# A hybrid decoder layer on one core: the first output projection moves behind the paired products, and eight more gates are computed in pairs

## The chip, the cores and the metric

The kernel runs on one core of a Trainium2 chip. The metric is the device time of one execution in microseconds, the median of three runs. The engines are called by the profile's names: PE is TensorE (matmuls; PEld its weight loads), DVE is VectorE, ACT is ScalarE, POOL is GpSimd and SP is SyncE, which here only issues DMAs. POOL issues DMAs too.

## The reference

One inference step of one layer, for a prompt of 512 tokens and 8 single sample tokens, 520 columns in all, at a model width of 2048:

```
sh1, sc1, g1, sh2, sc2, g2 = ada_mod(c, w_ada, b_ada)        # silu(c) @ w_ada + b_ada, split in six
h = modulate(rmsnorm(x, norm1_w), sh1, sc1)
mq, mk, mv, mo, mi, mf, fq, fk, fv, ff, ga, gb = split(h @ w_in + b_in)
y_m = mlstm_output(mlstm(mq, mk, mv, mi, mf), mo, m_hnorm_w)  # 4 heads, width 1024
y_f = forgetting_attention(rmsnorm(fq), rmsnorm(fk), fv, ff)  # 8 heads, width 1024, with a paged cache
merged = sigmoid(ga) * (y_m @ w_proj_a) + sigmoid(gb) * (y_f @ w_proj_b)
x = x + g1 * (merged @ w_out)
h2 = modulate(rmsnorm(x, norm2_w), sh2, sc2)
x = x + g2 * conv_ffn(h2)
```

All of it is in 32-bit floats. `ga` and `gb` are the two gates, 2048 rows each, that is 16 blocks of 128 rows each. y_m @ w_proj_a is the first projection.

## The kernel before, in words

**Layout.** Activations lie with features on the 128 partitions and the 520 columns in the free dimension. A product keeps 32-bit accuracy by splitting both operands into a rounded high part and the rest (`wh`, `wl` of a weight; `hh`, `hl` or the two halves of one tile of an activation), and by three matmuls: high by high, high by low, low by high.

**Two ways to multiply.** `dense` (line 197) computes one block of 128 output rows: for each 128 of the input features it issues 3 x 2 matmuls of 260 columns, 96 for an input width of 2048 and 48 for 1024. Each 1024 columns of weights are loaded by SP into a `raw` tile (seven buffers), cast by ACT into `wh`, and subtracted by DVE into `wl` (three buffers each). `Pair` (line 246) computes two blocks of 128 rows over 2048 features at once, as a 2 by 2 by 2 block product by Winograd's scheme: 7 products of 24 matmuls, 168 in all, where two dense blocks take 192. For that DVE adds weight tiles (four sums a pair) and splits seven weight forms, and the activations are needed in seven forms, `hX[1]` to `hX[7]`. The order of a pair's products is 1, 5, 6, 3, 7, 2, 4.

**What sets the order.** `run_pairs` (line 326) writes the order of the pairs out by hand, with a table of late steps at numbered products. In the dense stretches a list `bg` holds small steps; `dense` runs one of them after each 128 input features (`step`), and one entry of a list `pending` at some of its weight splits (`due`). Elsewhere a scheduler places the instructions of each engine, in an order that is then fixed: each engine, and the DMA queue of SP and of POOL, runs its list in order and waits where an operand or a buffer isn't ready.

**The stages around the change**, with the names that the change touches:

1. The start: the condition's products `ada` (a third of `w_ada` at once), the norm, and a first part `pre` of the projections.
2. The first mixer (mLSTM): 14 dense blocks over `h`, with the four heads' steps as `bg`. The last head's steps `m_tokens` and `m_out` (line 1178) run on into two blocks of the first gate (`w_gate`, line 1222), which only finish them. `m_out` leaves y_m as 16 resident tiles `ya`. From here `pending` holds the products of `w_ada` for SC2, two input blocks at a time.
3. The first projection, `pa`: 16 dense blocks over `ya` (line 1484). Two of them are multiplied by their gates by DVE; 14 are copied by ACT to tiles `pao` and stored by POOL to DRAM (`dmg`). After every second block `h_sums` (line 1242) builds the pairs' forms of one feature block: DVE adds high and low parts of `h` to `hu`, forms four sums, and splits them with ACT into `hf` tiles. Forms 5 and 6 stay; 7 and 4 go to DRAM (`dxf`) and are loaded again by POOL (line 1515, 16 DMAs) when the tiles of `ya` are free.
4. The pairs: 21 units, being 8 of queries and keys, 4 of values and 9 of gates: gate blocks 2 to 15 of `ga` and four of `gb`. A gate pair of `ga` loads the stored `pa` blocks (SP) and DVE multiplies them by the gates. SP loads and PE multiplies one block of `w_ada` for SH2 in each of 16 units (`late_load`, `late_product`).
5. The second mixer (forgetting attention): 12 dense blocks of `gb` (line 1762) as cover, 192 steps, under eight heads of attention and the sample tokens' cache: POOL gathers rows of keys `kp` and values `vp`, DVE multiplies and reduces `kp` to scores `sc`, and the attention's own chain runs over PE (`fS`, `fPT`, `fy`), DVE (`fs`, `sm`) and ACT. The gates' blocks leave through ACT (bias, `sgm`) and a store by POOL (`dsg`).
6. The second projection, `pb`: 16 dense blocks over `yf` (line 1939). The gates come back from `dsg`, 12 of them get their sigmoid here, and the sum with `dmg` becomes `merged`.
7. w_out in pairs, and the feed-forward, in pairs too.

## Time and profile before

| what | value |
|---|---|
| median of 3 runs | 2859.26 us (2858.5 to 2859.64) |
| the profiled execution, its own time | 2862.7 us |
| its span | 2861.0 us |
| PE busy in the span | 2825.4 us, 99% |
| DVE busy | 2154.0 us, 75% |
| ACT busy | 1360.5 us, 48% |
| POOL busy | 413.3 us, 14% |
| mean granted clock of PE | 0.997 |
| moved by DMA | 531.44 MB, mean 186 GB/s |

A row of the windows view gives a stretch of the span, and for each engine the busy time in it with the number of instructions that start there; then the granted clock as a share of full speed, the busy share of the DMA engines, and GB/s. A row of the timeline has a start, a duration, engine, line, operation, output and inputs, and in brackets the idle time before it and what ended that. A row of a tile's view has minimum, median and maximum duration in ns. Matmuls overlap, so a matmul's duration is longer than the step from one to the next.

### The profile page before, as it was taken

What the parts mean: (1) busy time and instruction counts of PE and PEld (TensorE: products, weight loads), DVE (VectorE), ACT (ScalarE), POOL (GpSimd) and SP (SyncE); (2) the same over time, 40 slices, a digit from 0 to 9 for tenths busy, and PEclk for the clock granted to TensorE, in tenths of its full rate; (3) what the DMA queues carried; (4) which work ended last, traced back from release to release, by engine and by line L of the source; (5) the groups of instructions that cost most, each with busy time, mean ns of one, the idle gap of its engine ahead of it and who ended that gap; (6) DMA issues with size and microseconds to landing.
All of it is one profiled execution on the core that took longest, in us unless ns stands there. A gap on an engine that the chain in (4) does not pass through costs nothing.

```text
span 2861.0 us, 57607 instructions
## 1 busy us (share of the span) xinstructions
PE 2825.4 (99%) x23318; PEld 2711.8 (95%) x23318; DVE 2154.0 (75%) x3318; ACT 1360.5 (48%) x2131; POOL 413.3 (14%) x687
## 2 busy tenths in 40 slices
PE   8999999999999999999999999999999999999999
PEld 6888998999999989799999999999999999999999
DVE  5986764676777759468888887878787888788787
ACT  4335543455455544444555444444444445544543
POOL 0001110211100145402111010101010101100100
PEclk9999999999999999999999999999999999999999
DMA  9946657945555578576772344444343346745753
GB/s 339 308 143 201 232 178 261 302 166 188 195 182 175 182 246 270 183 235 208 216 249 93 127 143 129 156 130 159 129 146 117 127 141 188 208 155 169 189 160 104
DMA packets 226755, 531.44 MB, mean 186 GB/s; under 512 B 30304, under 2 KB 83024, under 8 KB 226488
## 3 DMA queue, kind: packets, MB, share of 16 engines
q1 hardware_dynamic: 187296, 426.89, 46.2%
q0 software_dynamic: 38752, 100.64, 11.5%
q8 instruction: 183, 3.00, 0.4%
q14 instruction: 84, 0.69, 0.1%
q10 hardware_dynamic: 440, 0.23, 0.0%
HBM read 451.28 MB, written 72.92 MB: 183 GB/s over the span
## 4 chain that ended last, share of the span: by engine, by line
PE 85%; DVE 5%; issue 5%; DMA 2%; ACT 2%; POOL 1%; SPq 0%; POOLq 0%; DVEq 0%; ACTq 0%
PE x L60 33%; PE y L60 17%; PE z L60 8%; PE gate L213 4%; PE pre L60 3%; PE fo L60 3%; PE pa L213 3%; PE mo L213 2%; PE adp L60 2%; PE mv L213 2%; PE adp L409 1%; DVE wl L60 1%; PE mq L213 1%; PE mk L213 1%; ACT wh L60 1%
## 5 line engine op out<-in xcount | busy, mean ns | idle before, releaser
L60 DVE TENSOR_TENSOR wl<-raw,wh 128x1024 fp32r<-128x1024 f32 (+1 forms) x666 | 802.1, 1205 | 353.3 <-ACT wh L60 348.6
L60 ACT CAST wh<-raw 128x1024 fp32r<-128x1024 f32 (+1 forms) x666 | 689.5, 1036 | 754.7 <-DVE raw L60 386.3
L60 PE MATMUL x<-bf,wh 128*128 128x260 f32 x2624 | 475.2, 282 | 2.1 <-DVE tg L60 2.1
L60 DVE TENSOR_TENSOR raw<-raw,raw 128x1024 f32<-128x1024 f32 x339 | 413.7, 1220 | 5.8
L60 PEld LDWEIGHTS x<-bf,wh 128*128 128x128 f32 x2624 | 403.3, 188 | 2.2 <-ACT wh L60 2.2
L60 PE MATMUL x<-bf,wl 128*128 128x260 f32 x1312 | 370.0, 282 | 0.0
L60 PEld LDWEIGHTS x<-bf,wl 128*128 128x128 f32 x1312 | 246.8, 188 | 0.0
L60 PE MATMUL y<-bf,wh 128*128 128x260 f32 x1312 | 238.2, 282 | 0.0
L60 PEld LDWEIGHTS y<-bf,wh 128*128 128x128 f32 x1312 | 201.6, 188 | 0.0
L168 DVE TENSOR_TENSOR wl<-raw,wh 128x1024 fp32r<-128x1024 f32 x92 | 113.1, 1229 | 107.8 <-ACT wh L167 105.0
L60 PE MATMUL x<-ff,wh 128*128 128x260 f32 x1024 | 186.1, 283 | 0.0
L60 PE MATMUL x<-hf,wh 128*128 128x260 f32 x1008 | 185.4, 284 | 0.0
L60 PE MATMUL y<-bf,wl 128*128 128x260 f32 x656 | 184.7, 282 | 0.0
L167 ACT CAST wh<-raw 128x1024 fp32r<-128x1024 f32 x92 | 96.4, 1048 | 162.0 <-DMA raw<-in_w_in 43.4
L60 PEld LDWEIGHTS x<-hf,wh 128*128 128x128 f32 x1008 | 155.0, 188 | 13.4 <-issue 7.5
L60 PEld LDWEIGHTS x<-ff,wh 128*128 128x128 f32 x1024 | 157.6, 188 | 0.0
L60 PE MATMUL x<-ff,wl 128*128 128x260 f32 x512 | 144.6, 282 | 0.0
L60 PE MATMUL x<-hf,wl 128*128 128x260 f32 x504 | 142.2, 282 | 0.0
L60 PE MATMUL fo<-fe,wh 128*128 128x260 f32 x768 | 125.6, 284 | 1.1 <-DVE fo L60 0.9
L60 PEld LDWEIGHTS y<-bf,wl 128*128 128x128 f32 x656 | 123.5, 188 | 0.0
L60 PE MATMUL z<-bf,wh 128*128 128x260 f32 x656 | 120.9, 284 | 0.0
L60 PEld LDWEIGHTS fo<-fe,wh 128*128 128x128 f32 x768 | 105.6, 188 | 2.5 <-DVE fo L60 2.1
(642 smaller groups left out, 7076.9 us busy)
## 6 DMA issues: line engine op xcount, KB each, us to landing
raw<-in_w_fi SPq DMA_DIRECT2D x176, 512.0 KB
raw<-in_w_in SPq DMA_DIRECT2D x155, 512.0 KB
ar<-in_w_ada SPq DMA_DIRECT2D x192, 256.0 KB
raw<-in_w_ada SPq DMA_DIRECT2D x96, 512.0 KB
raw<-in_w_fo SPq DMA_DIRECT2D x64, 512.0 KB
raw<-in_w_out SPq DMA_DIRECT2D x32, 512.0 KB
raw<-in_w_fo SPq DMA_DIRECT2D x32, 384.0 KB
dff<-cc POOLq DMA_DIRECT2D x44, 260.0 KB
```

Of the source, the lines that this page charges most:

```text
L60: return lambda *a, **k: self.tc.keep_in_program_order(getattr(self.eng, op)(*a, **k))
L167: S.copy(wh[:, :n], raw[:, :n])
L168: V.tensor_tensor(wl[:, :n], raw[:, :n], wh[:, :n].bitcast(F32), op=ALU.subtract)
L213: T.matmul(acc[:, z, :HN], a[:, o], b[:, z * HN:(z + 1) * HN], start=(k == 0 and i == 0), stop=(k == K - 1 and i == 2))
L409: ins = T.matmul(ps[32 * g:32 * g + 32, :], cs[:, k, :], w, start=first, stop=last, tile_position=(0, 32 * g))
```

## The change

- **The first projection** leaves its place ahead of the pairs. `m_out` now stores y_m to DRAM (`dya`, 16 DMAs of POOL), and the 16 `pa` blocks run in the second mixer as cover, behind four dense blocks of `gb`. Their operand comes back in 16 loads by POOL into the buffers of `h`, which is used last by the fourth of those blocks. The gates of `ga` go to DRAM as sigmoids (`dsa`), SP fetches them two blocks ahead (`fetch_a`), DVE multiplies them by the block, and POOL stores the product (`dmg`).
- **Eight more gates in pairs:** all of `gb` but four blocks (12 instead of 4), so 13 gate pairs and 25 units. The gate pairs neither load nor multiply `pa` any more. The dense blocks in the second mixer's cover are now 4 of `gb` (64 steps) and 16 of `pa` (128 steps), 192 steps as before.
- **The forms of the pairs** are built in the first mixer: `h_whole`, `h_sums` and `h_parts` for each of eight feature blocks, one call at every eighth step. The low parts are subtracted by POOL, no longer by DVE, and all four forms go to DRAM. Forms 5 and 6 are loaded during the last head's steps, 7 and 4 at the pairs' start.
- **SC2's products** leave the two gate blocks and the first projection and join SH2's in the pairs: 32 in place of 16, some from tiles `ar` of another pool with four DMAs each.

The matmuls of 128x260 fall from 21350 to 21254; no other count of PE changes.

```diff
     def step():
         f = bg.pop(0) if bg else None
         if f:
             f()
+        n_step[0] += 1
+        if side and n_step[0] % 8 == 0:
+            side.pop(0)()
...
-            ya.append(split(sp, "s", t, "ya"))
+            for g, p in enumerate(split(sp, "s", t, "ya")):
+                G.dma_start(dya[4 * H.i + 2 * e + g][:, :N], p[:, :N])
...
+    def h_whole(i):
+        hu[i] = [pt("hu") for _ in range(2)]
+        for t, c in zip(hu[i], (i, 8 + i)):
+            V.tensor_tensor(t[:, :N], h[c][0][:, :N].bitcast(F32), h[c][1][:, :N].bitcast(F32), op=ALU.add)
...
+    def h_parts(i):
+        b11, b12, b21, b22 = (t[:, o:o + HN] for t in hu.pop(i) for o in (0, HN))
+        for q, f in enumerate((b11, b22, b12, b21)):
+            t = pt("hf", F32R)
+            hi, lo = parts_of(t)
+            S.copy(hi, f)
+            G.tensor_tensor(lo, f, hi.bitcast(F32), op=ALU.subtract)
+            G.dma_start(dxf[8 * q + i][:, :N], t[:, :N])
+    def load_form(n):
+        for i in range(8):
+            t = st("hf", F32R)
+            G.dma_start(t[:, :N], dxf[8 * FORMS.index(n) + i][:, :N])
+            hX[n][i] = parts_of(t)
+    side += [on(f, i) for i in range(8) for f in (h_whole, h_sums, h_parts)]
...
-    pending += ada_steps(SC2)
-    calls[:] = 0, 1, 2
-    NB2 = 4
+    NG = 2
+    NB2 = 12
...
-                if g < KC:
-                    V.tensor_tensor(t, t, self.pa[e][:, o], op=ALU.mult)
-                G.dma_start((dmg[g] if g < KC else dsg[g - KC])[:, o], t)
+                G.dma_start((dsa[g] if g < KC else dsg[g - KC])[:, o], t)
...
+    slots = []
+    for u in range(1, len(units) - 3):
+        slots.append((7 * u + 3, 7 * u + 6, False))
+        if u > 2 and not isinstance(units[u], QueryPair):
+            slots.append((7 * u + 6, 7 * u + 10, True))
+    for q, (ta, tb, by_pt) in enumerate(slots[:2 * KC]):
+        late(ta, late_load, q, by_pt)
+        late(tb, late_product, q)
...
+    h = None
+    ya = [[hp.tile([P, 528], F32R, tag="hl", name=nm("ya")) for _ in range(2)] for _ in range(8)]
+    for i, ts in enumerate(ya):
+        for g, t in enumerate(ts):
+            G.dma_start(t[:, :N], dya[2 * i + g][:, :N])
...
+    for j in range(KC):
+        acc = dense(I["w_pa"][j], ya, "pa")
+        t = ga.pop(j)
+        V.tensor_tensor(z2(t), acc, z2(t), op=ALU.mult)
+        G.dma_start(dmg[j], t[:, :N])
+        fetch_a(j + 2)
```

Three places of the order follow. First, POOL at the start of the pairs, before: `dxf` and `hf` are the forms, `dmg` from `pao` the stores of the first projection.

```order
L1502 DMA dmg_5242<-pao_6630 128x520
L1258 DMA dxf<-hf_6647 128x520
L1258 DMA dxf<-hf_6651 128x520
L1515 DMA hf_6786<-dxf 128x520
L1502 DMA dmg_5242<-pao_6712 128x520
L1515 DMA hf_6788<-dxf 128x520
```

The same place after: `dya` are the last head's stores of y_m, `dsa` the store of the second gate block.

```order
L1528 DMA dsa_2514<-sgm_5627 128x520
L872 DMA lfg<-in_cache_logf,idx_l 128x8
L1191 DMA dya<-yah_5664 128x520
L1191 DMA dya<-yal_5665 128x520
L1191 DMA dya<-yah_5672 128x520
L1191 DMA dya<-yal_5673 128x520
L1528 DMA dsa_2514<-sgm_5784 128x520
L1235 DMA hf_5787<-dxf 128x520
```

The first reload of form 7 stood behind stores of forms and projections; it now stands behind the four stores of the last head's output and behind the store of the last gate block.

Second, POOL in the second mixer around the third and fourth gate block, before: `kp` are the gathers of keys, `fql` and `fkl` low parts of the attention's queries and keys.

```order
L868 DMA kp_12878<-in_cache_k,idx_2452 128x512
L225 TENSOR_TENSOR fql_12744<-fi_12479,fqh_12743 128x512
L225 TENSOR_TENSOR fkl_12748<-fi_12480,fkh_12747 128x512
L1767 DMA dsg_5547<-sgm_12751 128x520
L868 DMA kp_12959<-in_cache_k,idx_2456 128x512
```

The same place after: `ya` are the loads of the projection's operand. Ten more of them, alike, are left out between the last `ya` shown and the gather.

```order
L872 DMA kp_12924<-in_cache_k,idx_2452 128x512
L1787 DMA ya_13018<-dya 128x520
L1787 DMA ya_13019<-dya 128x520
L1787 DMA ya_13020<-dya 128x520
L229 TENSOR_TENSOR fql_12790<-fi_12525,fqh_12789 128x512
L1787 DMA ya_13021<-dya 128x520
L229 TENSOR_TENSOR fkl_12794<-fi_12526,fkh_12793 128x512
L1787 DMA ya_13022<-dya 128x520
L1782 DMA dsg_5450<-sgm_12797 128x520
L1787 DMA ya_13023<-dya 128x520
...
L872 DMA kp_13005<-in_cache_k,idx_2456 128x512
```

All 16 loads stand between two gathers of keys, and the gathers that follow wait behind them.

Third, DVE in the second mixer where the fifth cover block begins, before: `wl` is a weight's low part, `fvl` and `fpl` low parts of values and probabilities.

```order
L60 TENSOR_REDUCE sc<-kp_12781 128x4
L225 TENSOR_TENSOR fpl_13012<-fPT_13006,fph_13011 128x384
L225 TENSOR_TENSOR fpl_13026<-fPT_13022,fph_13025 128x256
L60 TENSOR_TENSOR kp_12878<-kp_12878,qb_12875 128x512
L60 TENSOR_TENSOR kp_12959<-kp_12959,qb_12957 128x512
L168 TENSOR_TENSOR wl_13302<-raw_13299,wh_13301 128x1024
L60 TENSOR_REDUCE sc<-kp_12878 128x4
L225 TENSOR_TENSOR fvl_13078<-vtp_13072,fvh_13077 128x384
```

And after: `ga` is a gate, multiplied by the block `pa`.

```order
L229 TENSOR_TENSOR fpl_13108<-fPT_13104,fph_13107 128x256
L60 TENSOR_REDUCE sc<-kp_12923 128x4
L60 TENSOR_TENSOR kp_12924<-kp_12924,qb_12921 128x512
L168 TENSOR_TENSOR wl_13395<-raw_13392,wh_13394 128x1024
L60 TENSOR_REDUCE sc<-kp_12924 128x4
L1800 TENSOR_TENSOR ga_13050<-pa_13054,ga_13050 128x520
L229 TENSOR_TENSOR fvl_13160<-vtp_13154,fvh_13159 128x384
L60 TENSOR_TENSOR kp_13005<-kp_13005,qb_13003 128x512
```

One multiplication of 520 columns per `pa` block stands on DVE between the attention's steps, and the first gather that was queued behind the loads is the second operand after it.

More of the change, by code (lines that the diff above doesn't have):

```diff
@@ new lines, in tile_hybrid_step, with run @@
+    assert len(slots) >= 2 * KC
+    for q, (ta, tb, by_pt) in enumerate(slots[:2 * KC]):
+        late(ta, late_load, q, by_pt)
+        late(tb, late_product, q)
+        if q % KC == KC - 1:
+            late(tb + 2, late_turn, (SC2, SH2)[q // KC])
+    t0 = 7 * (len(units) - 2)
+    late(t0 + 1, root_load)
+    late(t0 + 3, root_make)
+    late(t0 + 6, rows_load)
+    late(t0 + 8, rows_make)
+    late(t0 + 9, lambda: (hX.pop(5), f_load(heads[0])))
+    late(t0 + 13, f_norm, heads[0])
+    def run(fs):
+        for f in fs:
+            f()
@@ L1747, in tile_hybrid_step @@
         put(183 if hh < FH - 1 else 188, y_sample, hh)
-    def run(fs):
-        for f in fs:
-            f()
     assert not bg
```

149 lines of the change are left out of this document (65 added, 84 removed).

## The prediction

> **What bounds the kernel now.** The page comes first: it says which engine fills the span.
>
> ```profile
> span 2861.0 us, 57607 instructions
> PE 2825.4 (99%) x23318; PEld 2711.8 (95%) x23318; DVE 2154.0 (75%) x3318; ACT 1360.5 (48%) x2131; POOL 413.3 (14%) x687
> ```
>
> PE is busy for all but 35.6 us. A share over the whole span says nothing of single stages, so the windows view is cut at the stages' borders: the first mixer, the two gate blocks, the first projection, the pairs, the second mixer (from 22 us after its start) and the second projection.
>
> ```profile
> 193.60:422.50 228.90, 228.43 (x1770) 207.27 (x1770) 159.56 (x337) 123.43 (x227) 33.68 (x52) 1.00 0.61 198
> 422.50:450.00 27.50, 27.50 (x230) 24.35 (x229) 12.32 (x20) 10.67 (x13) 0.00 (x0) 1.00 0.61 204
> 450.00:555.30 105.30, 105.30 (x874) 95.86 (x873) 56.03 (x101) 38.29 (x64) 20.06 (x37) 1.00 0.83 275
> 555.30:1004.10 448.80, 448.80 (x3724) 433.20 (x3723) 321.56 (x351) 236.17 (x361) 58.82 (x110) 1.00 0.57 188
> 1026.00:1219.60 193.60, 187.47 (x1414) 168.67 (x1415) 128.86 (x315) 87.26 (x188) 92.20 (x90) 0.98 0.69 229
> 1219.60:1311.00 91.40, 91.40 (x769) 91.40 (x768) 69.64 (x113) 42.39 (x66) 11.25 (x22) 1.00 0.63 200
> ```
>
> In the stages that the change takes apart PE has no idle time at full clock; only the second mixer shows some, 6.1 us. So a matmul less is time less, unless a new wait takes it back. The chain of waits gives the pace inside stages, start and duration of merged pieces.
>
> ```profile
> 458.01 11.72 PE pa L213 x96
> 471.59 11.72 PE pa L213 x96
> 659.38 5.95 PE x L60 x48
> 680.66 5.95 PE x L60 x48
> 961.32 5.75 PE x L60 x48
> 981.42 5.75 PE x L60 x48
> ```
>
> Each piece marks the same point of a period. Two `pa` blocks with one step of SC2's products (two input blocks) take 13.58 us; a pair with one SH2 product takes 21.28; a late pair without one takes 20.10.
>
> **The change, term by term.** First PE's work.
>
> 1. The first projection's stage goes: -105.3 us. Its 768 matmuls reappear in the second mixer, where they replace the 768 of eight gate blocks one for one: 0.
> 2. The gate blocks lose two SC2 steps. The second projection has 16 blocks in 91.4 us, 11.43 for two, so a step costs 13.58 - 11.43 = 2.15 us: -4.3.
> 3. Four more pairs, 4 x 20.1 = +80.4.
> 4. SC2's 16 products in the pairs at 21.28 - 20.10 = 1.18 each: +18.9.
>
> The sum is -10.3 us. Against it stand waits that can be new, at four places.
>
> **The first mixer.** The forms' building moves here. The prices are in the tile views (min, median, max in ns), in the groups of POOL, in the timeline where DVE and POOL run side by side, and in the ten-us windows, of which the first and the last of eight crowded ones stand here.
>
> ```profile
> L1246 DVE TENSOR_TENSOR hu<-hh,hl x16: 690/693/695, 442.7 to 545.8; 128x520 f32<-128x520 f32 x16
> L1248 DVE TENSOR_TENSOR hu<-hu x8: 420/422/423, 445.1 to 546.4; 128x260 f32<-128x260 f32 x8
> L225 POOL TENSOR_TENSOR fkl<-fi,fkh 128x512 fp32r<-128x512 f32 x8 | 10.3, 1287 | 0.0
> 1083.65 0.68 DVE L60 TENSOR_TENSOR kp<-kp,qb 128x512 f32<-128x512 f32 x1
> 1087.10 2.00 DVE L60 TENSOR_TENSOR kp<-kp,qb 128x512 f32<-128x512 f32 x2
> 1086.66 1.29 POOL L225 TENSOR_TENSOR fkl<-fi,fkh 128x512 fp32r<-128x512 f32 x1
> 210.00:220.00 10.00, 10.00 (x84) 8.27 (x84) 8.60 (x24) 2.94 (x4) 1.32 (x2) 1.00 0.73 263
> 400.00:410.00 10.00, 10.00 (x78) 9.75 (x77) 8.79 (x19) 6.21 (x17) 1.11 (x2) 1.00 0.53 170
> ```
>
> DVE gets eight blocks of 2 x 0.693 + 4 x 0.422, 24.6 us, over 192 steps. With 159.6 of 228.9 us busy it goes to 184, 80%. ACT gets 32 casts and has 105 us free. POOL gets 32 subtractions; scaled from 512 to 260 columns one is an estimated 0.65 us, 21 us in all, with 64 DMA issues that wait only for data. Two multiplications on DVE that POOL's subtraction overlapped took 2.00 us, not 2 x 0.68, so up to half of POOL's time can fall on DVE: 10 us, at the outside all 21, and then DVE is at 205 of 229, 90%. The cover is the three buffers of split weights, each some 6 us of PE. In eight of the ten-us windows DVE is busy for 8.5 us or more, between 8.53 and 9.79; adding 1.25 and 1.07 us to each overfills them by 10 us in sum. So the cost lies between 0 and 10 us. I take 0.5, near the low end, since PE waits nowhere in this stage now. Below 0 it can't go: there is no idle time to win.
>
> The Trainium skill ("SBUF — State Buffer", section "Who interferes with whom") says that a DVE instruction with two inputs in SBUF is shut out by a GpSimd instruction that reads SBUF, for the whole of it. The stretched pair above agrees. By that rule taken strictly the cost would be the outer end just named, and moving the subtractions to POOL would win DVE little; it is the first rival below.
>
> **The start of the pairs.** Form 7 is needed at the fifth product, 4 x 2.87 (20.10 / 7) = 11.5 us in, form 4 at the seventh, 17.2 us in, one tile each 0.36 us. The rows are POOL's first and last reload, the same stretch in the DMA view, DVE's `m_out`, and a reload of this sort before the next set of pairs.
>
> ```profile
> 550.55 0.55 POOL L1515 DMA_DIRECT2D hf<-dxf  x1
> 562.66 0.54 POOL L1515 DMA_DIRECT2D hf<-dxf  x1 [0.60 <-DMA hf<-dxf]
> DMA packets 3185, 7.00 MB, mean 333 GB/s; under 512 B 365, under 2 KB 365, under 8 KB 3182
> 438.62 0.76 DVE L363 SCALAR_TENSOR_TENSOR rv<-ms,rd 128x260 f32<-128x260 f32 x2
> 449.28 0.69 DVE L225 TENSOR_TENSOR yal<-hm,yah 128x520 fp32r<-128x520 f32 x1
> 1310.93 10.09 DMA mf<-dxf
> ```
>
> The reloads (16 x 266 KB, 4.26 MB) began 4.75 us ahead of the pairs at 555.3; in 550 to 571 the DMAs moved 7.0 MB at 333 GB/s. Now they stand on POOL behind the stores of `m_out`'s output and of the last gate. `m_out` ran from 438.6 to 450.0, 11.4 us; the second gate block takes 11.4 us without SC2's step, so it ends about at the pairs' start, four issues of 0.55 and the gate's activation come next, and the reloads begin some 3 us in, 8 us later than now. At 277 GB/s (4.26 MB in the 15.4 us that the saturated stretch took) the last tile lands near 3 + 2 + 15.4 = 20.4 us, against a need at 17.2 + 7 x 0.36 = 19.7. Cost 0 to 8 us (all of the shift); I take 1. The same sort of reload before the output pairs took 10.1 us from issue to landing and held PE up for about 1 us. Behind the reloads on POOL stand the first query pair's stores, whose data come later still.
>
> **The pairs themselves.** DVE is at 72% and loses 28 multiplications; SP loses 14 loads of `pa` and gains SC2's weights, 16.8 MB over more than 400 us, some 40 GB/s on 188. Loads into `ar` tiles wait for stores of the unit before, and weight loads stand behind them on SP, but those are wanted two or more products later. Cost 0, bounded by one product, 2.87 us.
>
> **The second mixer.** Its rows: POOL around the third and fourth gate block (the `dsg` stores follow their ends), the MB that SP's queue moves in 1004.1 to 1219.6, the price of a multiplication by a block, DVE's load after that, and a spell of idle time.
>
> ```profile
> 1059.74 0.95 POOL L868 DMA_INDIRECT kp<-in_cache_k,idx  x1 [0.30 <-issue]
> 1064.14 0.59 POOL L1767 DMA_DIRECT2D dsg<-sgm  x1
> 1074.84 0.99 POOL L868 DMA_INDIRECT kp<-in_cache_k,idx  x1 [10.12 <-DVE fs L1579]
> 1077.70 0.57 POOL L1767 DMA_DIRECT2D dsg<-sgm  x1
> q1 hardware_dynamic: 11485, 27.60, 40.1%
> L1971 DVE TENSOR_TENSOR sgm<-pb,sgm x16: 690/693/700, 1225.6 to 1311.5; 128x520 f32<-128x520 f32 x16
> 1070.00:1140.00 70.00, 69.61 (x554) 66.96 (x553) 64.33 (x148) 34.19 (x75) 37.35 (x36) 1.00 0.80 265
> 1004.00:1010.00 6.00, 6.00 (x48) 5.66 (x47) 2.26 (x5) 5.21 (x9) 2.82 (x6) 1.00 0.74 241
> 1022.00:1028.00 6.00, 4.03 (x29) 3.31 (x28) 6.00 (x22) 3.33 (x8) 2.04 (x3) 1.00 1.02 391
> 1028.00:1034.00 6.00, 3.15 (x15) 3.15 (x16) 4.04 (x9) 1.88 (x4) 3.53 (x4) 0.65 0.90 280
> 1034.00:1040.00 6.00, 6.00 (x39) 5.84 (x39) 2.68 (x4) 3.66 (x8) 1.94 (x2) 0.78 0.56 185
> ```
>
> The loads of `ya` wait for PE's last reading of `h`, by the fourth gate block, from about 1062 to 1077. POOL reaches them after the gather at 1059.7 and then has nothing to do until 1074.8, so they fit where they are. Their 4.26 MB share the DMAs with 265 GB/s; at 333 in all, and 128 (27.60 MB in 215.5 us) for SP's queue, while POOL's own gathers wait behind, they take about 21 us from 1064, so the last is there near 1085. PE wants it seven eighths into the first `pa` block, some 7 us after 1077: a wait of about 1 us. The gathers behind them land later by up to that stretch, and DVE waits for those in its order.
>
> DVE also multiplies 16 blocks, 16 x 0.693 = 11.1 us. Eight fall into 1070 to 1140, where it is busy for 64.3 of 70 us: 64.3 + 8 x 0.69 = 69.9. That is full. What a late DVE costs stands in the windows from 1022 to 1040: 4.8 us idle, and the granted clock falls to 0.65 and 0.78 after it, so 83 matmuls start where 144 would at the pace of 1004 to 1010; at 0.125 us that is 7.6 us. I take 2.5 us for this stage, between -6.1 (all its present idle time, but DVE's and SP's rows at its start are unchanged) and 15.
>
> All terms: -10.3 + 0.5 + 1 + 0 + 2.5 = -6.3. The profiled execution took 2862.7 us, 3.4 above the median of the runs; its 2856.4 corresponds to 2853.0 on the median. 5.7 us, 0.2%, is about what a measurement of this kernel can tell from no change.
>
> **The rivals.**
>
> - *The first mixer becomes DVE's* (chance 0.07). For it: eight crowded windows and the stretched multiplications; against: no wait of PE there today and 20% of slack on DVE even with the forms. Price 10 in place of 0.5: 2853.0 + 9.5 = 2862.5.
> - *DVE overfills in the second mixer* (0.14). For it: 69.9 of 70 us; against: weights are split two and three blocks ahead. One more spell like the one at 1025 replaces the 2.5: 2853.0 + 7.6 - 2.5 = 2858.1; two of them make 2865.7.
> - *The forms come late* (0.07): 8 in place of 1, 2860.0. For it, the shift by 8 us against a slack of a few; against, the first tile is wanted only 11.5 us in.
> - *The projection's operand comes late, and the kernel is slower* (0.10). If POOL hangs in the key gathers in front (they wait for buffers that DVE frees, as in the 10.12 us at 1074.8) and reaches the `ya` loads only when the fourth gate block ends, PE waits for 21 of stream less the 7 that the first block needs anyway, 14 us, and 3 for the clock: 17 in place of 2.5, 2867.5. It decides when POOL is some 9 us late: 9 and 3 for the clock are the 6.3 and 5.7 us that lie between my sum and slower.
> - *The fewer matmuls save nothing*: excluded by the windows, since PE never waited in the pairs.
>
> **How the numbers follow.** My own case has 0.62 and a range of 2847 to 2855.5: the net of -10.3 with stalls of 2 to 6.5, or less if the mixer's own idle time shrinks. Of that 0.54 lies under 2853.5, faster, and 0.08 within 0.2%. The first three rivals, 0.28, end within 0.2%; the fourth, 0.10, slower. So 0.54, 0.36, 0.10. The range runs from 2846 to 2864, over my case and the first three rivals; left out are the late operand and the tails.
>
> **What would show it.** Right: no stage between 450 and the pairs; pairs 25 units long with PE busy throughout, near 548 us (448.8 + 80.4 + 18.9); the two gate blocks in about 23; 0 to 2 us of waits of PE for `hf` and `ya` each. Wrong: POOL's first reload of form 7 over 5 us after the pairs' start; the first `ya` load after the fourth gate block's middle; a dip of the granted clock in the second mixer beyond the one at its start; DVE above 90% in the first mixer with PE waiting for `wl`. If PE's time falls by other than 10 us, terms 1 to 4 are wrong; if it falls and the span doesn't, a wait is.

## The result, and the profile after

The changed kernel is slower: 2897.33 us as the median of four runs (2896.16 to 2903.63) against 2859.11 us, a ratio of 1.0138 with a 95% interval of 1.0121 to 1.0156. Run again later beside other kernels it gave 1.0124 (1.0107 to 1.0141). The forecast was 2853.0, faster; 2864 was the top of its range. The trace below is of the execution of 2903.63 us, the longest of the four; where a second number is given, it is from the trace of the later repeat (2895.93 us).

First the page of the changed kernel, the lines that answer to those of before.

```profile
span 2901.6 us, 57751 instructions
PE 2841.4 (98%) x23222; PEld 2717.9 (94%) x23222; DVE 2194.6 (76%) x3312; ACT 1363.6 (47%) x2141; POOL 480.7 (17%) x793
```

PE is busy for longer than before, 2841.4 us, with fewer matmuls. So part of what was lost is matmuls that ran slowly, and PE's idle time grew as well, from 35.6 to 60.2 us. The windows at the same stages say where: the first mixer, the two gate blocks, the pairs, the second mixer from 21 us after its start, and the second projection.

```profile
193.60:444.20 250.60, 239.39 (x1807) 216.62 (x1806) 195.37 (x388) 134.85 (x260) 83.54 (x127) 0.98 0.70 227
444.20:467.50 23.30, 23.30 (x196) 23.30 (x195) 10.29 (x13) 9.47 (x11) 5.73 (x10) 1.00 0.63 201
467.50:1024.00 556.50, 553.32 (x4536) 520.79 (x4536) 374.78 (x388) 278.70 (x422) 72.35 (x136) 0.99 0.60 197
1045.00:1257.00 212.00, 197.22 (x1414) 172.93 (x1414) 137.00 (x330) 83.02 (x181) 104.66 (x114) 0.95 0.78 260
1257.00:1348.90 91.90, 91.90 (x771) 91.90 (x770) 70.58 (x114) 37.24 (x57) 11.71 (x22) 1.00 0.62 202
```

The first mixer is 21.7 us longer than before (5 of these are the start's: the mixer's first matmul, of `mo`, comes at 198.7 us, before at 193.7), the gate blocks 4.2 shorter, the first projection's 105.3 are gone, the pairs are 107.7 longer (99.3 were forecast), the second mixer from the end of the pairs to the second projection takes 233 in place of 215.5, 17.5 longer. Three stages lost what the matmuls gained.

In the first mixer PE now waits, in few and long pieces. These are its waits between 193.6 and 444.2 (waiting line, what for, us in total, times, longest).

```profile
PE ms L390 <- DVE hi L381: 4.5, 1, 4.5
PE ms L390 <- ACT hf L1228: 2.3, 1, 2.3
PE ktp L1151 <- DVE dl L1039: 1.9, 1, 1.9
```

They are the mixer's own chains: `ms` sums the squares in `m_out`, `ktp` turns the keys. What may stand in front of them is one queue further back, in SP's waits and in DVE's for the state (`c`, loaded by SP at line 1108, after; line 1105 before). SP's waits in the first mixer after:

```profile
SPq L1108 <- POOL hf L1229: 6.2, 1, 6.2
SPq L1108 <- DMA dxf<-hf: 4.6, 2, 3.0
SPq L1102 <- DMA dxf<-hf: 3.0, 2, 2.7
```

DVE's wait for that load, first after, then before:

```profile
DVE tmp L1111 <- DMA c<-in_state_C: 20.9, 8, 5.1
```

```profile
DVE tmp L1108 <- DMA c<-in_state_C: 8.1, 9, 1.6
```

The forms' tiles `hu` and `hf` come from the same nine buffers as the mixer's state, so SP can't load the state until a form has been stored, and DVE stands in its order until the state is there. These rows don't show how much of this reaches PE; the experiments below ask that.

A wait can cost more than its length. The windows around the one at 329 us show it; the last three columns are granted clock, DMA share and GB/s.

```profile
328.00:332.00 4.00, 1.46 (x11) 1.07 (x9) 3.15 (x12) 3.12 (x7) 1.18 (x2) 1.00 0.35 126
332.00:336.00 4.00, 3.97 (x19) 3.88 (x20) 3.96 (x6) 3.11 (x5) 3.98 (x5) 0.57 0.32 62
336.00:340.00 4.00, 4.00 (x34) 3.72 (x32) 3.67 (x5) 3.99 (x9) 3.31 (x4) 1.00 0.90 266
```

2.5 us of idle time, then four microseconds in which PE is busy but starts 19 matmuls in place of 34.

In the second mixer PE's waits are these:

```profile
PE sO L1701 <- DMA vp<-in_cache_v,idx: 6.9, 6, 5.3
PE fPT L1609 <- DVE fs L1598: 5.0, 2, 3.6
PE pa L217 <- DMA ya<-dya: 2.7, 5, 0.9
```

The second row was there before (5.2). The first is new at this size (0.4 before): the sample tokens' attention (`sO`) waits for gathered values. In POOL's timeline just ahead of that wait, the eight gathers in a row cut to their first and last:

```profile
1181.84 0.59 POOL L1801 DMA_DIRECT2D dmg<-ga  x1 [2.61 <-DVE ga L1800]
1182.55 1.28 POOL L229 TENSOR_TENSOR fql<-fi,fqh 128x512 fp32r<-128x512 f32 x1
1183.79 1.27 POOL L229 TENSOR_TENSOR fkl<-fi,fkh 128x512 fp32r<-128x512 f32 x1
1185.22 1.00 POOL L872 DMA_INDIRECT vp<-in_cache_v,idx  x1 [0.16 <-issue]
...
1194.59 0.97 POOL L872 DMA_INDIRECT vp<-in_cache_v,idx  x1 [0.30 <-issue]
```

A store of the first projection (`dmg`) waits for DVE's multiplication, and the gathers stand behind it on POOL. POOL's waits of this kind add up, in 1024 to 1257:

```profile
POOL dmg L1801 <- DVE ga L1800: 34.2, 6, 9.9
```

### The profile page after: what moved, and what is told of

Its sections match the earlier page's. It is cut to its first block, busy times and chain, and to the rows that moved or that the text cites. A ratio compares the mean times of both kernels' runs of the same rounds, so it can differ in the third digit from the quotient of the medians.

```text
span 2901.6 us, 57751 instructions
## 1 busy us (share of the span) xinstructions
PE 2841.4 (98%) x23222; PEld 2717.9 (94%) x23222; DVE 2194.6 (76%) x3312; ACT 1363.6 (47%) x2141; POOL 480.7 (17%) x793
## 5 line engine op out<-in xcount | busy, mean ns | idle before, releaser
L60 DVE TENSOR_TENSOR wl<-raw,wh 128x1024 fp32r<-128x1024 f32 (+1 forms) x694 | 837.0, 1207 | 384.7 <-ACT wh L60 379.0
L60 ACT CAST wh<-raw 128x1024 fp32r<-128x1024 f32 (+1 forms) x694 | 718.7, 1037 | 800.0 <-DVE raw L60 395.3
L60 DVE TENSOR_TENSOR raw<-raw,raw 128x1024 f32<-128x1024 f32 x355 | 433.6, 1221 | 6.1
L60 PE MATMUL x<-hf,wh 128*128 128x260 f32 x1200 | 221.7, 285 | 2.6 <-DMA hf<-dxf 2.6
L60 PEld LDWEIGHTS x<-hf,wh 128*128 128x128 f32 x1200 | 185.2, 189 | 20.3 <-issue 10.1
L60 PE MATMUL x<-hf,wl 128*128 128x260 f32 x600 | 169.9, 283 | 0.4 <-DVE wl L60 0.4
L167 ACT CAST wh<-raw 128x1024 fp32r<-128x1024 f32 x76 | 79.5, 1047 | 120.8 <-PE pa L217 36.3
L168 DVE TENSOR_TENSOR wl<-raw,wh 128x1024 fp32r<-128x1024 f32 x76 | 95.4, 1256 | 42.0 <-ACT wh L167 35.3
L2121 POOL COPY stc<-stc 128x8 f32<-128x8 f32 x44 | 8.3, 189 | 685.7 <-DVE cc L60 685.7
```

The source lines that it names most:

```text
L60: return lambda *a, **k: self.tc.keep_in_program_order(getattr(self.eng, op)(*a, **k))
L167: S.copy(wh[:, :n], raw[:, :n])
L168: V.tensor_tensor(wl[:, :n], raw[:, :n], wh[:, :n].bitcast(F32), op=ALU.subtract)
L2121: G.tensor_copy(stc[:, f, 0, :], stc[:, f, 1, :])
```

## The experiments

The table has every kernel that ran: the ratio to the runs of before made beside it, with its interval, the place where the first gate block's matmuls begin (before that lie the start and the first mixer), the length of the pairs, and that of the second mixer, from the pairs' last matmul to the second projection's first. Unedited stages show the scatter: the first gate block at 440.0 to 444.6 and a second mixer of 226.6 to 233.6 where neither code nor queue there was edited. What follows the second projection took 1549 to 1557 us in all of them; that scatter is not explained. In the diffs, `...` stands for code that is left out.

| kernel | ratio | first gate block at | pairs | second mixer |
|---|---|---|---|---|
| before | 1 | 422.6 | 448.9 | 215.6 |
| changed | 1.0138 (1.0121 to 1.0156) | 444.3 | 555.7 | 233.6 |
| changed, once more | 1.0124 (1.0107 to 1.0141) | 440.6 | 555.5 | 230.3 |
| all suspects left out | 0.9968 (0.9956 to 0.9980) | 422.2 | 549.8 | 217.5 |
| forms not computed | 1.0030 (1.0005 to 1.0055) | 422.5 | 555.4 | 229.6 |
| subtraction on DVE | 1.0081 (1.0055 to 1.0108) | 436.4 | 556.3 | 229.8 |
| small steps | 1.0093 (1.0075 to 1.0112) | 438.6 | 554.7 | 230.4 |
| own buffers | 1.0089 (1.0072 to 1.0106) | 432.2 | 555.6 | 226.6 |
| own buffers, three edits | 1.0064 (1.0047 to 1.0081) | 432.5 | 554.6 | 219.5 |
| the same, small steps | 1.0072 (1.0055 to 1.0089) | 433.9 | 555.7 | 219.7 |
| own buffers, ACT copies | 1.0071 (1.0055 to 1.0088) | 430.7 | 555.1 | 230.8 |
| own buffers, placed steps | 1.0065 (1.0047 to 1.0083) | 433.4 | 556.8 | 218.9 |
| state loaded by POOL | 1.0058 (1.0039 to 1.0078) | 436.9 | 553.2 | 216.1 |
| state in large buffers | 1.0122 (1.0105 to 1.0140) | 448.9 | 556.0 | 218.7 |
| no loads of y_m | 1.0094 (1.0067 to 1.0120) | 444.6 | 555.9 | 228.3 |
| no multiplication | 1.0079 (1.0054 to 1.0105) | 442.6 | 555.3 | 222.8 |
| small steps, late product | 1.0060 (1.0043 to 1.0078) | 439.6 | 554.6 | 219.7 |
| the same, y_m early | 1.0115 (1.0097 to 1.0134) | 437.0 | 555.4 | 232.0 |
| stores two blocks later | 1.0088 (1.0071 to 1.0105) | 440.0 | 555.4 | 219.2 |
| stores by ACT | 1.0100 (1.0083 to 1.0117) | 441.9 | 555.8 | 222.7 |

### Are the matmul terms right?

```diff
-        V.tensor_tensor(z2(t), acc, z2(t), op=ALU.mult)      # first projection
+        S.copy(z2(t), acc)
-    ya = [[hp.tile(...) ...]]; G.dma_start(t[:, :N], dya[...])
+    ya = h[:8]
-        load_form(n)                                         # n = 7, 4
+        hX[n] = [parts_of(h[i][0]) for i in range(8)]
-            S.copy(hi, f); G.tensor_tensor(lo, f, hi, ...)   # and h_whole, h_sums
+            G.dma_start(dxf[8 * q + i][:, :N], h[...][:, :N])
```

> Leaves out all four suspected costs at once: the computing of the forms, the reloads of forms 7 and 4 (their products read tiles of h instead), the loads of y_m and the multiplications by the first gate (values wrong, PE's matmuls all there). Theory (the prediction's four matmul terms were right, and all of the loss is these waits and the half clock behind them): first gate block at 422 to 423, the two gate blocks 23.5, the pairs 548 to 550, the second mixer 215 to 218, the whole 8 to 12 us under before, 0.996 to 0.997. Rival (the SC2 products by way of `ar` tiles, or the four more pairs, cost more than the terms): pairs of 553 to 556 also without the reloads, the whole at 0.9985 to 1.000.

The ratio is 0.9968 (0.9956 to 0.9980): of 2859.3 us that is 9.2 us less, between 5.7 and 12.6. The windows of this kernel, for the first mixer, the gate blocks, the pairs and the second mixer:

```profile
193.60:422.20 228.60, 227.81 (x1762) 206.43 (x1762) 159.76 (x337) 121.65 (x228) 33.99 (x62) 1.00 0.65 209
422.20:445.80 23.60, 23.60 (x199) 23.60 (x198) 10.67 (x14) 9.85 (x11) 8.20 (x15) 1.00 0.74 234
445.80:995.60 549.80, 549.23 (x4530) 517.52 (x4529) 373.74 (x387) 277.82 (x420) 64.50 (x120) 1.00 0.59 192
995.60:1213.10 217.50, 208.50 (x1583) 188.95 (x1582) 138.35 (x340) 99.78 (x215) 108.71 (x112) 0.98 0.79 260
```

By these windows the stage that is gone, the gate blocks and the pairs give -105.3, -3.9 and +101.0, together -8.2 us: the sum of the four terms, -10.3, is borne out to within some 2 us. All of the loss against before is in what was left out here.

### The first mixer: computing, buffers, amount or place?

```diff
     def h_whole(i):
-        hu[i] = [pt("hu") ...]; V.tensor_tensor(t, hh, hl, op=ALU.add)
+        pass
```

> Leaves out the computing of the forms (no additions, sums, casts or subtractions); POOL stores parts of h in their place, so the 32 stores, the reloads and all matmuls stay and the forms' values are wrong. Theory (the computing on DVE, ACT and POOL overfills the first mixer): the first mixer with its lead-in goes from 444 back to within 3 us of 422.5, PE's waits there under 1.5 us, no half-clock spell there; the whole 2873 to 2878. Rival (POOL's issues, the stores' traffic and the stores of y_m cost it): the first mixer stays above 240 and the whole above 2888.

The first gate block begins at 422.5, as before the change, and PE's waits are gone (0.6 us are left), though all stores are still made. So the stores as such are not the cost; the computing is, together with the small buffers that it holds, which this run leaves free too.

```diff
-            G.tensor_tensor(lo, f, hi.bitcast(F32), op=ALU.subtract)
+            V.tensor_tensor(lo, f, hi.bitcast(F32), op=ALU.subtract)
```

> One edit to the changed kernel: the 32 subtractions of the forms' low parts run on DVE (an estimated 0.35 us each, 11 us in all, half of the 0.69 that a 520-column two-input instruction takes in the trace) in place of POOL (0.76 us each, 24.5 us in all). Theory A, POOL's subtraction shuts out DVE's two-input instructions, so that the forms cost DVE 24.6 + 24.5 us as it stands: the first mixer gets shorter by 5 to 13 us (250.6 to about 240), the whole about 2888. Theory B, DVE's own queue is overfull and POOL costs it little: the first mixer gets longer by up to 11 us, about 258, the whole 2900 to 2908. Theory C, it is the place of the steps in DVE's order and not the load: within 3 us of 2897.

The first gate block begins at 436.4 against 440 to 444.6, so 4 to 8 us earlier, and the whole is 12 to 16 us shorter by the ratios, whose intervals are some 8 us to each side. That is theory A's direction, at the lower end of its size. But 2.5 to 4.7 us of it lie in the start: the mixer's first matmul comes at 194.2, and at 196.7 to 198.9 where the first mixer is unedited; the mixer itself takes 242.2 us against 243.0 to 245.7, hardly clear of the scatter. In the start, where the first steps of the forms run, the timeline has the same small instruction of DVE in both kernels, changed kernel first:

```profile
168.98 1.09 POOL L1229 TENSOR_TENSOR hf<-hu,hf 128x260 fp32r<-128x260 f32 x1 [165.74 <-ACT hf L1228]
170.70 1.89 DVE L60 TENSOR_TENSOR x<-x,ada 128x8 f32<-128x8 f32 x1
171.12 1.44 POOL L1229 TENSOR_TENSOR hf<-hu,hf 128x260 fp32r<-128x260 f32 x2
```

```profile
170.18 0.15 DVE L60 TENSOR_TENSOR x<-x,ada 128x8 f32<-128x8 f32 x1
```

It lasts 0.15 us without POOL's subtractions, and 1.89 us with two of them, until they are done. In the changed kernel PE then waits 3.3 us for `pre`. POOL's subtraction takes this long (min, median, max in ns):

```profile
L1229 POOL TENSOR_TENSOR hf<-hu,hf x32: 733/764/1755, 169.0 to 413.4; 128x260 fp32r<-128x260 f32 x32
```

Then the same work in other portions, at steps where the mixer has none:

```diff
-        if side and n_step[0] % 8 == 0:
+        if side and not f and n_step[0] >= 16 and n_step[0] - n_step[1] >= 2:
+            n_step[1] = n_step[0]
             side.pop(0)()
```

> As the run with the subtraction on DVE, but the 24 steps of the forms are cut into 64 small ones (one or two DVE instructions each), which run only in steps that have no work of the mixer, two steps apart and from the sixteenth step on. DVE's work is the same. Theory 'place' (the lumps stand in DVE's order ahead of what PE waits for): the first mixer goes from 242.8 to 228 to 234, the lead-in loses its wait, whole ratio 1.003 to 1.006. Theory 'load' (196 us of DVE work don't fit into 229): it stays at 239 to 245, ratio 1.007 to 1.009.

The first gate block stays at 438.6: these places don't help. But this kernel's trace had DVE waiting for the state (21.3 us) and SP for stores of forms (15.3), which led to the buffers:

```diff
-        hu[i] = [pt("hu") for _ in range(2)]
+        hu[i] = [st("hu") for _ in range(2)]
-            t = pt("hf", F32R)
+            t = st("hf", F32R)
```

> One edit to the changed kernel: the forms' temporaries hu and hf come from the 33 large buffers (tag s) in place of the nine of tag p, which the mixer's state update takes too. The work on DVE, ACT and POOL is the same. Theory 'buffers' (SP's loads of the mixer's state wait for stores of hf, 16 us of such waits, and DVE in its order for those loads, 20.9 us against 8.1 before): DVE's waits for the state's loads fall to about 8 to 12 us, the first mixer goes from 250.6 to 230 to 240, the whole 10 to 20 us under the changed kernel. Theory 'load' (DVE's and POOL's work as such): the first mixer stays above 246.

Both parts came: the first gate block at 432.2, 8 to 12 us earlier with the same instructions, and the whole 10 us less by the ratios (1.0124 to 1.0089). DVE's wait for the state in this kernel, and behind it the same wait in the kernel with all suspects left out:

```profile
DVE tmp L1111 <- DMA c<-in_state_C: 9.4, 7, 2.9
```

```profile
DVE tmp L1111 <- DMA c<-in_state_C: 19.1, 8, 5.1
```

The second line warns against reading the gain off the first: there DVE waits 19.1 us for the state, and the first gate block begins at 422.2 all the same. So the sum of this wait is no measure of the cost. And the edit moved work as well: the first form's steps on DVE begin at 202.6 us in place of 165.5, so the wait of 3.3 us for `pre` in the start, which they had brought, is gone too. The mixer's first matmul comes at 193.0, 4 to 6 us earlier than where the first mixer is unedited, and the mixer itself takes 239.2 in place of 243.0 to 245.7 us. So about half of the gain lies in the start; the other half, 4 to 6 us, lies in the mixer and goes with the buffers or with the later steps that they brought. 9.6 us are left between 432.2 and 422.6. Three more edits went on top, each in another stage; here it is the subtraction on DVE that counts.

```diff
-            G.tensor_tensor(lo, f, hi.bitcast(F32), op=ALU.subtract)
+            V.tensor_tensor(lo, f, hi.bitcast(F32), op=ALU.subtract)
-                G.dma_start(dya[c][:, :N], p[:, :N])   # last head: kept
+    load_form(7); G.dma_start(dya[c][:, :N], p[:, :N]); load_form(4)
-        V.tensor_tensor(z2(t), acc, z2(t), op=ALU.mult)
+        S.copy(z2(t), acc)                 # product with dsa[j] at the second projection
```

> As the run before with three more edits, each in a stage of its own: the subtraction on DVE (first mixer), the multiplication by the gate in the second projection (second mixer), and the last head's stores of y_m on POOL behind the reload of form 7 in place of ahead of it (start of the pairs). Theory 'buffers' and 'lock': first mixer 228 to 234; the reload of form 7 begins 4 us earlier, PE's wait for hf goes from 2.6 to under 1 us and the pairs from 555.6 to 549 to 552; second mixer 219 to 221. The whole about 0.998 to 1.001. Theory 'load' for the first mixer: it stays at 239 to 244, the whole at 1.003 or more.

The first gate block begins at 432.5: with buffers of their own it doesn't matter which engine subtracts. The mixer stayed near theory 'load' (238.9 us, against 239 to 244), and the pairs at 554.6, above their range. The first-mixer windows of the two, own buffers first, say why the engine doesn't matter.

```profile
193.60:432.20 238.60, 230.57 (x1765) 208.37 (x1764) 189.99 (x385) 131.53 (x260) 90.20 (x138) 0.99 0.75 242
```

```profile
193.60:432.50 238.90, 231.33 (x1762) 208.86 (x1761) 187.65 (x416) 131.44 (x260) 63.44 (x101) 0.99 0.74 237
```

DVE runs 31 instructions more in the second, of 0.42 us each, 13 us, and is busy for 2.3 us less. So POOL's subtractions stretched DVE's other instructions by an estimated 15 us, of their own 24.5 (32 x 0.764). The Trainium skill ("SBUF — State Buffer", "Who interferes with whom") has a DVE instruction with two SBUF inputs contend with a GpSimd instruction that reads SBUF, and calls the contention an exclusive lock; the direction agrees, in the start above most plainly, and six tenths of POOL's time is what is seen over the mixer.

> As the run before, with the forms in 64 small steps at the steps without work of the mixer. Theory 'buffers': with the waits for buffers gone the small steps cost the least, first mixer 228 to 232, the whole 0.997 to 1.000. Theory 'load': no better than the run before, 239 to 246.

The first gate block begins at 433.9: small steps again win nothing. Two runs then took the amount and the place apart:

```diff
-            V.tensor_tensor(t[:, :N], h[c][0], h[c][1], op=ALU.add)
+            S.copy(t[:, :N], h[c][0])
```

> Forms' temporaries in buffers of their own and the subtraction on DVE, as in the run with the three further edits, but without the two in other stages; and the 16 additions of high and low part of h (0.69 us each, 11 us on DVE) are replaced by copies of the high part on ACT (the forms lack the low parts; everything else runs). Theory 'load' (what is left of the cost is the amount of DVE's work): first gate block from 432.5 to 423 to 427. Theory 'order' (DVE stands behind waits of its own in its order, and the amount matters little): 430 to 433.

```diff
+        while side and n_step[0] >= WHEN[len(WHEN) - len(side)]:
+            side.pop(0)()
```

> The forms in 64 small steps with all their work, on DVE, in buffers of their own, placed over all 224 steps of the first mixer in proportion to the idle time that DVE had at each stretch of eight steps in the run without the forms' computing (38 us of work into 71 us); and the gate's multiplication in the second projection, as before. Theory 'order': first gate block at 423 to 427, the whole 1.002 to 1.004. Theory 'load': 431 to 435, the whole at 1.006 to 1.008.

The first gate block begins at 430.7 and 433.4. 11 us less work on DVE, with copies on ACT in their place, give 1.5 to 1.8 us, less than the scatter, and work placed by DVE's idle time gives nothing. Last, the loads of the state were taken off SP's queue, or given other buffers:

```diff
-                nc.sync.dma_start(c3, I["state_C"][...])     # and qkb
+                G.dma_start(c3, I["state_C"][...])
```

> As the run with own buffers, the subtraction on DVE and the multiplication in the second projection; the mixer's 32 loads of state (16 of the state, 16 of q and k rows) are issued by POOL in place of SP, so that they no longer stand behind weight loads. Theory 'loop' (weights late, so SP's queue late, so the state's loads late, so DVE late): DVE's waits for the state fall from 12.8 to under 8 us, first gate block from 432.5 to 423 to 427, the whole 1.002 to 1.004. Rival (DVE's waits for the state fill time that it has to spare; what is late is late by its own work): 430 to 434, the whole at 1.006.

```diff
-                t = pt("qkb") ... c0 = pt("c0")
+                t = st("qkb") ... c0 = st("c0")
```

> As the run just named, but the state's loads stay on SP and get buffers from the 33 large ones. Theory 'loop by buffers' (SP waits for the nine small buffers also where the mixer's own tiles hold them, 6.3 us in the run with own buffers): first gate block at 424 to 428. Rival: 430 to 434.

The first gate block begins at 436.9 and 448.9, both worse in this stage. But neither run made the state come earlier: DVE's wait for it is 25.9 us with POOL as the issuer and 15.5 with the large buffers, against the 12.8 of the run that they start from. So the theory of a loop through SP's queue isn't confirmed, and it isn't refuted either, since what it needs did not come about. (The run with POOL as the issuer is nevertheless the lowest of the complete ones, though its interval overlaps those of others. Its pairs and second mixer, 553.2 and 216.1, are the short ones, where it has no edit beyond those above. At the start of its pairs PE waited 2.2 us for `hf`, and no slow clock followed; the rest isn't explained.) What the other half of this stage's cost is stays open; the runs show only that it goes with the computing as a whole, that it sits in one to three waits of 2 to 5 us for the mixer's chains and the slow clock behind them, and that neither the 11 us taken off DVE nor the places tried for the steps changed it beyond the scatter.

### The second mixer: loads, multiplications or POOL's queue?

```diff
-    ya = [[hp.tile([P, 528], F32R, tag="hl", name=nm("ya")) ...]]
+    ya = h[:8]
```

> Leaves out the 16 loads of y_m in the second mixer; the first projection reads eight tile pairs of h that are there already (wrong values, same matmuls; the stores stay). Theory (the loads come late and crowd out the gathers of keys): the second mixer goes from 233 to 216 to 222 us, the spells of idle time near 1085 to 1100 and their half clock are gone; the whole 2881 to 2886. Rival (DVE's 16 multiplications overfill it): 2893 to 2898.

```diff
-        V.tensor_tensor(z2(t), acc, z2(t), op=ALU.mult)
+        S.copy(z2(t), acc)
```

> Leaves out the 16 multiplications by the first gate on DVE (0.69 us each); ACT copies the block out in their place (the result lacks the first gate; the loads of the stored gates stay). Rival of the loads' theory (DVE overfull in the second mixer): the second mixer gets shorter by 8 to 15 us, the whole 2882 to 2889. Theory (the loads of y_m): by at most 4 us, 2893 to 2898.

Without the loads the stage takes 228.3, within the scatter of the unedited stage: PE's wait at the projection's start is gone, and one of 4.9 us comes at `sO`. (The whole, 1.0094, is 9 to 13 us lower by the ratios, but its interval overlaps that of the second unedited run; this run alone doesn't settle what the loads cost.) Without the multiplications it takes 222.8. So the multiplications cost 7.5 to 11 us; read so, DVE would be the bound. Moved to the second projection they give the same without leaving anything out:

> As the run with small steps, and the multiplication by the first gate moves from the second mixer to the second projection (ACT copies the block out, DVE multiplies it there in SBUF, 16 x 0.69 = 11.1 us into a stage where it is busy for 69.6 of 91.4; nothing is left out). Theory: second mixer 229 to 233 down to 221 to 224, second projection longer by 0 to 3, together 6 to 10 us less than with the small steps alone. Rival (the second projection is DVE's then): it gets longer by 8 or more and nothing is won.

The stage takes 219.7, against 230.4 with the small steps alone, and the second projection 92.4 against 92.3. Loading half of y_m earlier on top:

```diff
+        if j == KC - 1:
+            ya += [[st("ya", F32R) for _ in range(2)] for _ in range(4)]; load_ya(0, 4)
```

> As the run before, and the first 8 of the 16 tiles of y_m go into other buffers and are loaded ahead of the last gate block, so that only the other 8 wait for the tiles of h. Theory (PE's 4 us of waits at the start of the first projection and the half clock after them are the late loads): the wait goes to under 1 us and the second mixer gets shorter by 4 to 6 us, to 216 to 219. Rival (the loads collide with POOL's gathers, whose data the attention wants): the wait comes back at the gathers, change under 2 us.

The stage takes 232.0: the rival's way. The wait for `ya` fell to 1.1 us, but PE waited 4.7 us for POOL's `fkl` in the attention. The wait for `fkl` points at POOL's queue, and the run with the late product fits that too, since its stores no longer wait for DVE. So the last two runs keep every multiplication on DVE and move only the stores behind them:

```diff
-        G.dma_start(dmg[j], t[:, :N])
+        held.append((j, t))
+        while len(held) > (2 if j < KC - 1 else 0):
+            c, u = held.pop(0)
+            G.dma_start(dmg[c], u[:, :N])
```

> One edit to the changed kernel: POOL's store of a block of the first projection is issued two blocks (11 us) later, when its multiplication is long done. Theory 'queue' (the gathers of values stand on POOL behind stores that wait for DVE): POOL's waits for the products fall from 34 to under 8 us, PE's wait of 5.3 us for vp goes, the second mixer goes from 230 to 233 down to 222 to 225, as with the multiplication left out. Theory 'DVE' (its 11 us of work): 229 to 233.

```diff
-        G.dma_start(dmg[j], t[:, :N])
+        S.dma_start(dmg[j], t[:, :N])
```

> One edit to the changed kernel: the same stores are issued by ACT. Theory 'queue': the second mixer at 222 to 226, unless ACT's own waits for the products hold up its casts of weights (then PE waits for wh, and it stays near 230). Theory 'DVE': 229 to 233.

The stage takes 219.2 and 222.7, against 230.3 and 233.6 in the unedited kernel's two traces. This is the window of the second mixer with the stores two blocks later, and PE's waits in it:

```profile
1018.90:1238.00 219.10, 208.80 (x1582) 189.47 (x1581) 147.90 (x355) 92.67 (x199) 117.95 (x128) 0.98 0.84 278
```

```profile
PE fPT L1609 <- DVE fs L1598: 5.6, 3, 3.9
PE pa L217 <- DMA ya<-dya: 4.1, 7, 1.0
PE sS L1666 <- DVE sc L1659: 0.5, 1, 0.5
```

All multiplications are still on DVE (147.9 us busy), PE still waits for the loads of y_m (4.1), and the stage is 11 to 14 us shorter; `sO` no longer waits. By the wholes only the stores two blocks later are clear of both unedited runs; the interval of the stores by ACT overlaps the second. The loads are in this run, and it is within 1.7 us of the kernel with all suspects left out (217.5): with the stores out of the way they and the multiplications cost little. The stage came out below the range of the expectation (222 to 225), and one number missed, POOL's waits for the products (in 1019 to 1254, 16 us beyond the stage; within it 19.3):

```profile
POOL dmg L1805 <- DVE ga L1801: 25.2, 5, 8.7
```

They were to fall from 34.2 to under 8. So it isn't the sum of the stores' waits that counts; read with `sO`, what counts is whether gathers that PE will want stand behind them.

> The changed kernel once more, unedited, beside the others on the same chip: a control. Expected 1.0138 within the interval, first mixer 250 to 251, pairs 555 to 556.5, second mixer 231 to 234.

This control came out as expected but for the first mixer, 247.0, and the second, 230.3, just under its range, and so gives the scatter: 4 us in the first mixer and 3 in the second between two profiles of one kernel.

## Why the prediction was wrong, point by point

- **Terms 1 to 4 were right** to within some 2 us. Gate blocks -4.2 (-4.3 forecast); the stage gone -105.3; pairs 549.8 without the reloads (548.1). The kernel with all suspects left out is 9.2 us faster than before, against the sum of 10.3. That matmuls were worth their time was never the weak point.
- **The first mixer's term failed**: 0.5, bounds 0 to 10, measured 18 to 22 with the start. The step that failed is the bound itself, which asked only whether DVE's time within the mixer would suffice. Its inputs were near: POOL's subtraction 0.76 us (0.65 estimated), some 15 us of it on DVE (10 in the estimate), DVE busy for 195.4 us of the stage (up to 205 forecast). Yet DVE was far from full, 78% of the longer stage. Not counted were two things. The forms' first steps run in the start, where POOL's subtractions held up DVE (1.89 us in place of 0.15) and PE waited for `pre`: the mixer began 3 to 5 us later than before. And `hu` and `hf` share nine small buffers with the mixer's state. With own buffers, and the later steps that came with them, 8 to 12 us went, some half of it in the start. The remaining 9.6 have no cause that an experiment confirmed. The signs named for this (DVE above 90%, PE waiting for `wl`) did not come either; the cost came by another door.
- **The second mixer's term failed**: 2.5, bounds up to 15, measured 14.7 and 18.0 (230.3 and 233.6 against 215.6). The step that failed is the reckoning of DVE's 69.9 of 70 us, which took DVE's time for what a multiplication costs, and beside it the step on the operand, which followed POOL's queue for the loads of y_m only. The 16 stores behind the multiplications are on POOL too, each waits for DVE in its order, and the gathers of values stand behind them. With these stores later the stage takes 219.2, 3.6 over before, and with all suspects out 217.5, 1.9 over: about the 2.5 that was forecast. The loads of y_m began at 1081.7, 13 us ahead of the projection at 1094.9, and the last was issued at 1100.4; PE waited 2.7 to 4.1 us for them, not 1, and a slow clock followed (0.77 in 1102 to 1106, 0.65 in 1106 to 1110): the sign named for it, a dip of the clock beyond the one at the start, came. As to the rivals, the late operand (17 for this stage) and DVE overfull with two spells (15.2) both gave the right order of size for a wrong reason: what was late is POOL's gathers behind the stores, not the loads, and DVE kept its work in the run that was short.
- **The start of the pairs**: 1, bounds 0 to 8, measured 5.7 (555.5 against 549.8). POOL's first reload of form 7 began at 472.1, 4.6 us in, not 3, and form 4 was late. The windows from there on:

```profile
480.00:484.00 4.00, 3.61 (x31) 3.40 (x30) 3.72 (x5) 2.06 (x3) 1.89 (x4) 1.00 1.12 376
484.00:488.00 4.00, 3.40 (x27) 2.99 (x25) 3.34 (x5) 1.56 (x2) 0.00 (x0) 1.00 1.09 364
488.00:492.00 4.00, 2.01 (x7) 1.50 (x8) 1.91 (x2) 0.00 (x0) 0.00 (x0) 0.68 1.11 376
492.00:496.00 4.00, 4.00 (x20) 4.00 (x20) 0.00 (x0) 1.36 (x3) 0.00 (x0) 0.50 0.05 16
```

  The place (seventh product, 17.2 us in) and the price (wait for the saturated DMAs) were right, the reload's length was taken too short: the DMAs are full until about 491, 24 us in and 19 us after the first reload in place of 15.4, with weights beside the forms. Of the 5.7 us, 2.6 to 3.2 are waits for `hf`, and the slow clock makes an estimated 3.3 at the most (4 us each at 0.68 and 0.50). Placing y_m's last stores behind form 7 in the program changed little (554.6), since POOL reached the reloads only 2.5 us earlier and the transfers stayed as long.
- **The chances.** Each place had a price, but they were weighed as rivals of each other. All three happened at once, and the first mixer went beyond its bound.

No kernel here beats before: the best that leaves nothing out is at 1.0058 (1.0039 to 1.0078). Own buffers together with the later stores weren't run.

## What to carry to other kernels

Work that moves into a stage takes its buffers and its places in queues along, not only its time on an engine: ask whose loads wait for the buffers that it takes, and which transfers stand behind each of its stores. An engine that is 78% busy, or a wait that is long in sum, says nothing by itself; an engine that runs its list in order passes a wait on to whatever is next in line. A change of buffers also moves work in time, so look where the steps went before calling the buffers the cause. And when several places can each cost something, price the case that all of them do.

## What the runs showed of the hardware

Short waits of PE were often followed by about half the clock. After one of 2.3 us at 329 and one of 0.3 behind it, four microseconds had a granted clock of 0.57; at the start of the pairs no wait was longer than 1.33 us, yet the clock was 0.68 in the window that holds this wait and 0.50 in the next. In the run with the state loaded by POOL, waits of 2.2 us in sum at the same place, none over 0.9, left it at 1.00. The Trainium skill ("TensorE: Matmul & The Clock Gate", Part 1) has the clock fall after an idle window of about 3.4 us; no wait there is as long as that, so here the clock fell sooner.
